# An mLSTM stage whose decay exponents are stored head by head, with their exponentials computed on ScalarE instead of stored and loaded

## The chip, the cores and the metric

The kernel runs on one core of one Trainium2 chip. The metric is the device time of one execution in microseconds (us); a profiled execution has in addition a span, from its first to its last instruction. The engines are named as in the profile: PE is TensorE, PEld its weight loads, DVE is VectorE, ACT is ScalarE, POOL is GpSimd, SP is SyncE (here it only issues DMAs).

## What is computed

One step of a hybrid backbone with a single trunk layer: RMSNorm, one combined input projection, multi-head latent attention beside a bidirectional chunkwise mLSTM, a gated merge, an output projection and a SwiGLU feed-forward part. There are 128 context tokens and 1024 latent tokens, model width 1024. The part that matters here is the mLSTM scan, with 4 heads, key width 128 and value width 256, once forward and once backward:

```python
b = cumsum(fc); log_d = where(mask, b[:, None] - b[None, :] + ic[None, :], -inf)
inter = b + m
m_row = maximum(inter, max(log_d, -1))
d = exp(log_d - m_row)
w_inter = exp(inter - m_row)
s = (q @ k.T) * d
num = s @ v + w_inter * (C @ q)
den = sum(s) + w_inter * (n @ q)
h = num / maximum(abs(den), exp(-m_row))
...
decay = exp(b_last + m - m_new)
C_new = decay * C + einsum(w, v, k)
```

The kernel does this in chunks of 128 tokens. For one token, with the chunk's own running sum taken out, it needs one exponent per head, `N` (minus the row maximum), from which `d` is exp(N + mask + a value per key), and `w_inter` is exp(N + mr), where `mr` is one number per direction, head and chunk.

## The kernel before, in words

All matrices lie transposed, features on partitions. Float32 products that need it are made of three fp32r matmuls (`mm3`, lines 98 to 100), whose high and low parts ACT (`hi`, L69) and DVE (`lo`, L75) split. The program runs through an input stage with 24 big projection tiles (`z_big`), the mLSTM stage (`z2`), the attention, the merge and the feed-forward part. Instructions stand on each engine in the order that the framework's scheduler gave them at build time; each engine works through its list in order and waits where a semaphore isn't there yet. SP's list of DMA issues is in order too.

**The gates** (`gates`, lines 748 to 840) run in the background of the input stage. They hold one row per direction, head and chunk (100 rows with gaps), 128 tokens along the free axis. `N` is computed on DVE (L818), `E` = exp(N + mr) on ACT (L819), and four DMAs (L822) write both for both directions into the DRAM tensor `d_nm`, whose order is [N or E, direction, head, chunk, token]. A diagonal matrix `Z` with the state decay is spread over all partitions by one matmul with ones (L839) and copied to `dec` (L840). `tok` holds other per-token numbers, transposed.

**The mLSTM stage** (`z2`, lines 982 to 1041) takes 18 steps i = 0 to 17, forward and backward chunks in turn; the first two (the context) carry no state in, the other 16 are "carried". Each step has these parts:
- `mload` (L1043), three steps ahead: loads `N` (L1047, one row of 128 tokens per head, spread to all 128 partitions: 256 KB), `S` (L1049: scores and keys, 512 KB), `V` (L1054) at a chunk's first use, and for a carried step `Q` (L1057) and `W` (L1059: the exponentials `E` out of `d_nm`, spread like `N`, 256 KB). The loads of i = 0 are issued by POOL, all others by SP. `N` and `W` have three buffers each.
- `mfront` (L1062), one step ahead: POOL adds the mask to `N` in place (L1072) and multiplies `Q` by `W` (L1074), ACT takes the exponential of `N` for each head (L1077), POOL scales the keys (L1079), DVE multiplies the result by the scores (L1081).
- `mback` (L1084): per head the matmuls L1102 (`N` with `V`), L1104 (`Q` with the state `C`) and L1107 (state update), two instructions each; DVE updates `C` (L1109) and takes the denominators (L1120 to L1122); ACT (L1127, first visit of a chunk) or DVE (L1125, second visit) takes the output out of PSUM.
- `mpost` (L1132): norm, transposes and gating of a finished chunk.

Between these stand pieces of the attention's key, value and query projections (`proj`, `fill`), whose PSUM results ACT copies to `st` tiles (L896, L920, L942). They use two PSUM banks with the tag `mm`. The first `st` tile takes over a buffer from which `z_big` has just stored its last result (`d_z<-zo`, L684).

Of the kernel before, what the change touches and what calls it, by code (L numbers as in the profile page):

```python
# [10 lines left out]
F32 = mybir.dt.float32  # L11
R32 = mybir.dt.float32r
I32 = mybir.dt.int32
AF = mybir.ActivationFunctionType
ALU = mybir.AluOpType
# [4 lines left out]
P = 128  # L20
# [5 lines left out]
NCH = T // P  # L26
CW = 384
CHUNKS = [(i * CW, CW) for i in range(T // CW)]
HM = 4
# [17 lines left out]
NR = 100  # L47
# [9 lines left out]
class K:  # L57
# [107 lines left out]
    def build(self):  # L165
        tc, nc, a, o = self.tc, self.nc, self.a, self.o
        with tc.tile_pool(name="const", bufs=1) as cp, \
                tc.tile_pool(name="dr", bufs=1, space=DRAM) as dp:
            self.cp, self.dp = cp, dp
            self.ident = cp.tile([P, P], F32, name="ident")  # L170
            make_identity(nc, self.ident)
            self.ones = cp.tile([P, P], F32, name="ones")
            nc.gpsimd.memset(self.ones, 1.0)
            self.vec = cp.tile([P, 64], F32, name="vec")
            self.mod1 = cp.tile([P, 16, 2], F32, name="mod1")
            self.mod2 = cp.tile([P, 4, 8, 2], F32, name="mod2")
            self.A1 = cp.tile([P, 8, 2], F32, name="A1")
            self.A2 = cp.tile([P, 8, 2], F32, name="A2")
            self.silc = cp.tile([P, 8, 2], F32, name="silc")
            self.dram()  # L180
            self.bm = cp.tile([P, 48], F32, name="bm")
            self.tok = cp.tile([P, 3, NR], F32, name="tok")
            self.dec = cp.tile([P, NR], F32, name="dec")
            self.inputs()
            self.attention()
            self.merge()
            self.ffn()
# [4 lines left out]
    def dram(self):  # L192
        t = self.dp.tile
        self.d_q = t([NCH, P, HM, P], F32, name="d_q")
        self.d_v = t([NCH, P, HM, DV], F32, name="d_v")
        self.d_s = t([NCH, P, 2, HM * P], F32, name="d_s")
        self.d_sp = t([P, T], F32, name="d_sp")
        self.d_nm = t([2, 2, HM, NCH, P], F32, name="d_nm")
        self.d_lat = t([5, P, T], F32, name="d_lat")
        self.d_z = t([24, P, T], F32, name="d_z")  # L200
        self.d_hm = t([KD, P, T], F32, name="d_hm")
        self.d_qn = t([HA * NOPE, T], F32, name="d_qn")
        self.d_qr = t([HA * ROPE, T], F32, name="d_qr")
        self.d_ko = t([HA * NOPE, NK], F32, name="d_ko")
        self.d_vo = t([HA, P, NCH + 1, AV], F32, name="d_vo")
        self.d_kpe = t([ROPE, T], F32, name="d_kpe")
        self.d_att = [t([P, 2, T], F32, name=f"d_att{k}") for k in range(4)]
        self.d_t2 = t([KD, P, T], F32, name="d_t2")
        self.d_x1 = t([KD, P, T], F32, name="d_x1")
        self.d_w = t([KD // 2, 4, P, HK * P], F32, name="d_w")  # L210
        self.d_g = t([NF, P, T], F32, name="d_g")
# [536 lines left out]
    def gates(self):  # L748


        nc, a, o, pp = self.nc, self.a, self.o, self.pp
        V, S = nc.vector, nc.scalar
# [6 lines left out]
        dirs = ((slice(0, 36), 1, P - 1), (slice(64, 100), -1, 0))  # L759
        I, F, A, U, L, Z, N, E = (g() for _ in range(8))  # L760
        sel, sm, GB, SB = g(17), g(1, 8), g(2), g(18)
        gb, mn, mc = g(18, 8), g(9, 8), g(9, 8)
        mr, nl, dd = g(1), g(1), g(1)
# [6 lines left out]
        for kd, t in enumerate((I, F)):  # L770
            for d in range(2):
                r = 32 * kd + 4 * d
# [43 lines left out]
        V.tensor_scalar(L, F, mr, None, op0=ALU.max)  # L816

        V.tensor_scalar(N, L, -1.0, None, op0=ALU.mult)  # L818
        S.activation(E, N, AF.Exp, bias=mr)  # L819
        for j, t in enumerate((N, E)):  # L820
            for d in range(2):
                nc.sync.dma_start(self.d_nm[j, d].rearrange("h c t -> (h c) t"), t[dirs[d][0]])  # L822
        V.scalar_tensor_tensor(A, A, -1.0, L, op0=ALU.mult, op1=ALU.subtract)
        S.activation(A, A, AF.Exp)
        yield
# [3 lines left out]
        S.activation(U, I, AF.Exp, bias=nl)  # L829
        S.activation(dd, nl, AF.Exp, bias=mr)  # L830
        V.tensor_scalar(Z[:, 0:NR], self.ident[0:NR, 0:NR], dd, None, op0=ALU.mult)
        yield
        yield
        tp = self.bank(pp, "mx")
# [1 line left out]
            nc.tensor.transpose(tp[:, i * NR:(i + 1) * NR], t, self.ident[0:NR, 0:NR])  # L836
        V.tensor_copy(self.tok, tp[:, 0:3 * NR].rearrange("p (g r) -> p g r", g=3))
        db = self.bank(pp, "mx")
        nc.tensor.matmul(db[:, 0:NR], self.ones[0:NR], Z[:, 0:NR], start=True, stop=True)  # L839
        S.copy(self.dec, db[:, 0:NR])  # L840

    def lat_kv(self):

# [199 lines left out]
    def mload(self, i, d, c, carried, second, mp):  # L1043
        nc = self.nc
        eng = nc.gpsimd if i < 1 else nc.sync
        N = mp.tile([P, HM, P], F32, name=self.nm("N"), tag="N", bufs=3)
        eng.dma_start(N, self.d_nm[0, d, :, c].partition_broadcast(P))  # L1047
        S = mp.tile([P, 2, HM * P], F32, name=self.nm("S"), tag="S", bufs=3)
        eng.dma_start(S, self.d_s[c])  # L1049
        Q = W = None  # L1050
        if c not in self.Vt:
            V = self.Vt[c] = mp.tile([P, HM, VW], F32, name=f"V{c}", tag=f"V{c or 3}")
            nc.gpsimd.memset(V[:, :, DV:VW], 1.0)
            eng.dma_start(V[:, :, 0:DV], self.d_v[c])  # L1054
        if carried:
            Q = mp.tile([P, HM, P], F32, name=self.nm("Q"), tag="Q", bufs=3)
            eng.dma_start(Q, self.d_q[c])  # L1057
            W = self.wp.tile([P, HM, P], F32, name=self.nm("W"), tag="ws", bufs=3)
            eng.dma_start(W, self.d_nm[1, d, :, c].partition_broadcast(P))  # L1059
        return S, N, Q, W  # L1060

    def mfront(self, d, c, carried, second, S, E, Q, W):  # L1062

        nc = self.nc
        G = nc.gpsimd
        r = 64 * d + c
        h4 = lambda t: t.rearrange("p (h t) -> p h t", h=HM)
        last = c == (NCH - 1 if d == 0 else 1)
        K = None if last else h4(S[:, 1])

        def work():
            G.tensor_tensor(E, E, self.neg[:, d:d + 1, :].broadcast_to([P, HM, P]), op=ALU.add)  # L1072
            if carried:
                G.tensor_tensor(Q, Q, W, op=ALU.mult)  # L1074
            yield
            for h in range(HM):
                nc.scalar.activation(E[:, h], E[:, h], AF.Exp, bias=self.tok[:, 2, r + 9 * h:r + 9 * h + 1])  # L1077
            if not last:
                G.tensor_tensor(K, K, self.tok[:, 1, r:r + 28:9].unsqueeze(2).broadcast_to([P, HM, P]), op=ALU.mult)  # L1079
            yield  # L1080
            nc.vector.tensor_mul(E, E, h4(S[:, 0]))  # L1081
        return work(), (E, Q, K)

    def mback(self, d, c, carried, second, A, Q, K, C, mp, pp, side, load):  # L1084
# [12 lines left out]
        for h in range(HM):  # L1097
# [7 lines left out]
            if K is not None:  # L1105
                p3 = self.bank(pp, "p3")[:, :VW]
                self.pe = mm(p3, K[:, h], V[:, h], start=True, stop=True).ins  # L1107
                if carried:
                    nc.vector.scalar_tensor_tensor(C[:, r], C[:, r], self.dec[:, r0 + 9 * h:r0 + 9 * h + 1], p3,  # L1109
                                                   op0=ALU.mult, op1=ALU.add)  # L1110
                else:
                    nc.scalar.copy(Co[:, h], p3)
# [983 lines left out]
```

## Time and profile before

| quantity | value |
|---|---|
| time, median of 3 runs (lowest to highest) | 2212.89 us (2212.23 to 2213.59) |
| profiled execution: its own time, and its span | 2207.67 us, 2205.9 us |
| mean granted TensorE clock | 0.967 of 2.4 GHz |
| busy, share of the span: PE, PEld | 93%, 85% |
| busy, share of the span: DVE, POOL, ACT | 69%, 45%, 42% |
| bytes moved by DMA, mean rate | 343.89 MB, 156 GB/s |
| DMA packets, of them under 2 KB | 233794, 166734 |

PE is busy nearly all the time, so time is lost only where PE stands or runs at the lower of its two clock levels. A busy share is a mean over stages: the mLSTM stage, from about 628 to 828 us of the span, has limits of its own. An engine's wait is put down by the trace to the releaser that came last; the DMA engines' share counts the time of packets, and can be a little over 1.

### The profile page before, as it was taken

What the parts mean: (1) busy time and instruction counts of PE and PEld (TensorE: products, weight loads), DVE (VectorE), ACT (ScalarE), POOL (GpSimd) and SP (SyncE); (2) the same over time, 40 slices, a digit from 0 to 9 for tenths busy, and PEclk for the clock granted to TensorE, in tenths of its full rate; (3) what the DMA queues carried; (4) which work ended last, traced back from release to release, by engine and by line L of the source; (5) the groups of instructions that cost most, each with busy time, mean ns of one, the idle gap of its engine ahead of it and who ended that gap; (6) DMA issues with size and microseconds to landing.
All of it is one profiled execution on the core that took longest, in us unless ns stands there. A gap on an engine that the chain in (4) does not pass through costs nothing.

```text
span 2205.9 us, 36808 instructions
## 1 busy us (share of the span) xinstructions
PE 2052.1 (93%) x13495; PEld 1870.1 (85%) x13495; DVE 1531.2 (69%) x2688; ACT 933.2 (42%) x1850; POOL 1002.3 (45%) x774
## 2 busy tenths in 40 slices
PE   5899989999989988999999999889999999989897
PEld 2589989989978775667677899879999999989897
DVE  5737746989844877556665647899655555899895
ACT  4433334455445544333443335544322222456464
POOL 1702223667524414444445535577777733521501
PEclk8899999999999997999999999899999999999899
DMA  7323334555489785222224664223555512557664
GB/s 297 105 96 103 105 104 152 167 164 187 147 264 317 233 265 168 73 69 75 81 75 119 201 207 148 79 88 130 182 178 193 177 61 84 176 166 251 220 200 131
DMA packets 233794, 343.89 MB, mean 156 GB/s; under 512 B 20078, under 2 KB 166734, under 8 KB 232462
## 3 DMA queue, kind: packets, MB, share of 16 engines
q1 hardware_dynamic: 225070, 331.88, 47.1%
q0 software_dynamic: 4848, 6.06, 1.1%
q10 hardware_dynamic: 3696, 3.61, 0.5%
q8 instruction: 106, 1.74, 0.3%
q14 instruction: 74, 0.61, 0.1%
HBM read 253.69 MB, written 87.80 MB: 155 GB/s over the span
## 4 chain that ended last, share of the span: by engine, by line
PE 45%; DVE 12%; DMA 8%; POOL 7%; issue 6%; ACT 2%; SPq 1%; DVEq 0%; POOLq 0%; ACTq 0%
PE mm L98 11%; PE mm L100 11%; PE mm L99 10%; DVE wo L75 4%; PE pv L1476 3%; DMA pr<-w_fo 3%; PE st L98 2%; PE st L99 1%; PE st L100 1%; PE mx L1398 1%; DMA wr<-w_fo 1%; DVE sm L1400 1%; PE p L1102 1%; POOL ps L1773 1%; POOL wm L722 1%
## 5 line engine op out<-in xcount | busy, mean ns | idle before, releaser
L100 PE MATMUL mm<-th,wo 128*128 128x288 f32 x1840 | 546.9, 298 | 14.2 <-DVE wo L75 13.9
L98 PE MATMUL mm<-th,wo 128*128 128x288 f32 x1840 | 547.8, 298 | 2.8 <-DVE zo L1702 1.1
L99 PE MATMUL mm<-tl,wo 128*128 128x288 f32 x1840 | 546.3, 297 | 0.0
L100 PEld LDWEIGHTS mm<-th,wo 128*128 128x128 f32 x1840 | 349.1, 190 | 18.4 <-DVE wo L75 17.9
L75 DVE TENSOR_TENSOR wo<-wr,wo 128x512 fp32r<-128x512 f32 (+1 forms) x317 | 313.1, 1003 | 57.5 <-ACT wo L69 52.9
L98 PEld LDWEIGHTS mm<-th,wo 128*128 128x128 f32 x1840 | 348.4, 189 | 4.8 <-issue 1.9
L99 PEld LDWEIGHTS mm<-tl,wo 128*128 128x128 f32 x1840 | 348.7, 190 | 0.1
L69 ACT ACTIVATE wo<-wr 128x512 fp32r<-128x512 f32 (+1 forms) x317 | 187.5, 608 | 145.8 <-PE mm L100 66.7
L75 DVE TENSOR_TENSOR wo<-ws,wo 128x512 fp32r<-128x512 f32 x188 | 188.2, 1004 | 64.4 <-ACT wo L69 64.3
L69 ACT ACTIVATE wo<-ws 128x512 fp32r<-128x512 f32 x188 | 116.5, 626 | 270.2 <-PE mm L100 152.1
L1445 POOL TENSOR_TENSOR es<-es,p 128x512 f32<-128x512 f32 x112 | 157.3, 1404 | 91.0 <-ACT p L1438 87.0
L100 PE MATMUL mm<-xh,wo 128*128 128x288 f32 x616 | 184.1, 300 | 9.7 <-DVE wo L75 9.7
L98 PE MATMUL mm<-xh,wo 128*128 128x288 f32 x616 | 183.8, 299 | 0.7 <-ACT wo L69 0.7
L99 PE MATMUL mm<-xl,wo 128*128 128x288 f32 x616 | 184.4, 300 | 0.0
L1686 POOL TENSOR_TENSOR ws<-wr,ws 128x512 f32<-128x512 f32 x47 | 62.3, 1326 | 226.1 <-DVE wo L75 220.8
L1438 ACT ACTIVATE p<-st 128x512 f32<-128x512 f32 (+1 forms) x152 | 87.5, 579 | 157.9 <-PE st L100 143.2
L1400 DVE TENSOR_REDUCE sm<-mx 128x1 f32<-128x384 f32 (+1 forms) x200 | 99.2, 540 | 66.1 <-PE mx L1398 65.3
L98 PE MATMUL mm<-B,wo 128*128 128x288 f32 x456 | 134.8, 296 | 2.4 <-DVE zo L1702 1.5
L100 PE MATMUL mm<-B,wo 128*128 128x288 f32 x456 | 134.8, 296 | 0.0
L99 PE MATMUL mm<-B,wo 128*128 128x288 f32 x456 | 134.7, 295 | 0.0
L722 POOL TENSOR_TENSOR wm<-wm,sr 128x512 f32<-128x512 f32 x64 | 100.9, 1579 | 64.6 <-DVE mj L721 61.6
L100 PEld LDWEIGHTS mm<-xh,wo 128*128 128x128 f32 x616 | 117.9, 192 | 11.8 <-DVE wo L75 11.6
(438 smaller groups left out, 5072.9 us busy)
## 6 DMA issues: line engine op xcount, KB each, us to landing
wr<-w_ff SPq DMA_DIRECT2D x56, 512.0 KB
wm<-wm SPq DMA_DIRECT2D x32, 512.0 KB
wr<-d_w SPq DMA_DIRECT2D x32, 512.0 KB
d_z<-zo SPq DMA_DIRECT2D x48, 288.0 KB
d_g<-uu SPq DMA_DIRECT2D x44, 288.0 KB
wr<-w_big SPq DMA_DIRECT2D x24, 512.0 KB
wr<-w_fo SPq DMA_DIRECT2D x24, 512.0 KB
pr<-w_fo SPq DMA_DIRECT2D x40, 256.0 KB
```

Of the source, the lines that this page charges most:

```text
L69: i = self.nc.scalar.activation(out, in_, AF.Copy)
L75: return self.nc.vector.tensor_sub(out, in_, f32v(hi)).ins
L98: mm(out, lhs[0], rhs[0], start=first, stop=False)
L99: mm(out, lhs[0], rhs[1], start=False, stop=False)
L100: self.pe = mm(out, lhs[1], rhs[0], start=False, stop=last).ins
L722: nc.gpsimd.tensor_tensor(w[:, n], w[:, n], sr[:, 1], op=ALU.mult)
L1102: self.pe = mm(p1, A[:, h], V[:, h], start=True, stop=not carried).ins
L1400: self.iv = nc.vector.tensor_reduce(sm[:, t, j:j + 1], s[:, :kc], axis=AX.X, op=ALU.max, negate=True).ins
L1438: self.ia = nc.scalar.activation(p[:, :n], st[:, :n], AF.Exp).ins
L1445: nc.gpsimd.tensor_tensor(U["sum"], U["sum"], p, op=ALU.add)
L1476: self.pe = nc.tensor.matmul(pv[g * AV:(g + 1) * AV, q0:q0 + w], v[:, kb[c]], U["P"][c][:, q0:q0 + w], start=c < 2, stop=c == U["nc"] - 1, ...
L1686: G.tensor_tensor(s4, a12, s2, op=ALU.subtract)
```

## The change

Four things, in one edit:
- `d_nm` becomes [direction, chunk, head, token], `N` alone. Eight DMAs (one per direction and head, 9 rows each) store it instead of four (36 rows each, two for `N` and two for `E`). The load of a step's `N` then reads one run of 2 KB for each partition instead of four of 512 B.
- `E` is no longer computed on ACT in the gates, stored, or loaded. `W` stays as a buffer, without a DMA.
- The gates spread `mr` over the partitions as well: a second diagonal matrix on DVE, a second matmul with ones, and a copy of 200 columns to `dec`, which now has two planes.
- In `mfront` of a carried step, ACT first computes `W` = exp(N + mr) for each of the four heads, from `N` as loaded; the mask is added to `N` in place after that.

```diff
-            self.dec = cp.tile([P, NR], F32, name="dec")
+            self.dec = cp.tile([P, 2, NR], F32, name="dec")
...
-        self.d_nm = t([2, 2, HM, NCH, P], F32, name="d_nm")
+        self.d_nm = t([2, NCH, HM, P], F32, name="d_nm")
...
         V.tensor_scalar(N, L, -1.0, None, op0=ALU.mult)
-        S.activation(E, N, AF.Exp, bias=mr)
-        for j, t in enumerate((N, E)):
-            for d in range(2):
-                nc.sync.dma_start(self.d_nm[j, d].rearrange("h c t -> (h c) t"), t[dirs[d][0]])
+        for d in range(2):
+            for h in range(HM):
+                r = 64 * d + 9 * h
+                nc.sync.dma_start(self.d_nm[d, :, h], N[r:r + NCH])
...
         V.tensor_scalar(Z[:, 0:NR], self.ident[0:NR, 0:NR], dd, None, op0=ALU.mult)
+        V.tensor_scalar(E[:, 0:NR], self.ident[0:NR, 0:NR], mr, None, op0=ALU.mult)
...
-        nc.tensor.matmul(db[:, 0:NR], self.ones[0:NR], Z[:, 0:NR], start=True, stop=True)
-        S.copy(self.dec, db[:, 0:NR])
+        for i, t in enumerate((Z, E)):
+            nc.tensor.matmul(db[:, i * NR:(i + 1) * NR], self.ones[0:NR], t[:, 0:NR], start=True, stop=True)
+        S.copy(self.dec, db[:, 0:2 * NR].rearrange("p (g r) -> p g r", g=2))
...
-        eng.dma_start(N, self.d_nm[0, d, :, c].partition_broadcast(P))
+        eng.dma_start(N, self.d_nm[d, c].partition_broadcast(P))
...
             W = self.wp.tile([P, HM, P], F32, name=self.nm("W"), tag="ws", bufs=3)
-            eng.dma_start(W, self.d_nm[1, d, :, c].partition_broadcast(P))
...
         def work():
+            for h in range(HM if carried else 0):
+                nc.scalar.activation(W[:, h], E[:, h], AF.Exp, bias=self.dec[:, 1, r + 9 * h:r + 9 * h + 1])
             G.tensor_tensor(E, E, self.neg[:, d:d + 1, :].broadcast_to([P, HM, P]), op=ALU.add)
...
-                    nc.vector.scalar_tensor_tensor(C[:, r], C[:, r], self.dec[:, r0 + 9 * h:r0 + 9 * h + 1], p3,
+                    nc.vector.scalar_tensor_tensor(C[:, r], C[:, r], self.dec[:, 0, r0 + 9 * h:r0 + 9 * h + 1], p3,
```

The scheduler makes its lists anew, so the change also moves instructions. After the edit the lines of `mfront` and below have numbers higher by three (L1077 is L1080, L1127 is L1130), those between `gates` and `mload` higher by two (L896 is L898, L1047 is L1049), and the new exponentials are L1074.

The first place is on ACT, where the steps i = 3, 4 and 5 begin (about 664 to 682 us of the trace). The exponents of i = 3, 4, 5 are `N_1030`, `N_1050`, `N_1066` in both programs; `st`, `kc` and `wh` belong to the projections, `h` is a step's output. Before:

```order
L896 COPY kc_1011_6625<-mm_1012_6626 128x128
L896 COPY st_1013_6634<-mm_1014_6635 128x288
L896 COPY st_1013_6634<-mm_1015_6643 128x288
L896 COPY st_1013_6634<-mm_1029_6694 128x288
L1077 ACTIVATE N_1030_6702<-N_1030_6702,tok_95 128x128 x2
L896 COPY st_1013_6634<-mm_1035_6718 128x288
L1077 ACTIVATE N_1030_6702<-N_1030_6702,tok_95 128x128 x2
L69 ACTIVATE wh_1078_6899<-wr_1006_6603 128x512
L896 COPY kc_1039_6747<-mm_1040_6748 128x128
L1077 ACTIVATE N_1050_6784<-N_1050_6784,tok_95 128x128 x4
L1127 ACTIVATE h_1089_6970<-p1_1092_6973,den_1091_6972 128x256 x2
L1127 ACTIVATE h_1089_6970<-p1_1101_7026,den_1091_6972 128x256 x2
```

And now:

```order
L898 COPY kc_1011_6630<-mm_1012_6631 128x128
L1074 ACTIVATE W_1033_6715<-N_1030_6706,dec_96 128x128 x4
L898 COPY st_1013_6639<-mm_1014_6640 128x288
...
L1074 ACTIVATE W_1053_6796<-N_1050_6787,dec_96 128x128 x2
L1080 ACTIVATE N_1030_6706<-N_1030_6706,tok_95 128x128 x4
L1074 ACTIVATE W_1053_6796<-N_1050_6787,dec_96 128x128 x2
L69 ACTIVATE wh_1078_6908<-wr_1006_6608 128x512
L898 COPY kc_1039_6750<-mm_1040_6751 128x128
L1080 ACTIVATE N_1050_6787<-N_1050_6787,tok_95 128x128 x4
L1074 ACTIVATE W_1069_6877<-N_1066_6868,dec_96 128x128 x4
L1130 ACTIVATE h_1089_6979<-p1_1092_6982,den_1091_6981 128x256 x2
L1130 ACTIVATE h_1089_6979<-p1_1101_7038,den_1091_6981 128x256 x2
```

The new exponentials of i = 3 stand ahead of the copies of `st`, two of i = 4 ahead of all four old exponentials of i = 3, and those of i = 5 ahead of the outputs `h`.

The second place is on SP, where the loads of the same steps are issued. Before:

```order
L223 DMA wr_6651<-w_uqn 128x384
L254 DMA d_ko<-st_6538 128x576
L1059 DMA W_6871<-d_nm 128x4x128
L254 DMA d_ko<-st_6538 128x576
L254 DMA d_ko<-kc_6577 128x128
L223 DMA wr_6897<-w_uqr 128x768
L1047 DMA N_6702<-d_nm 128x4x128
L1059 DMA W_6998<-d_nm 128x4x128
L1049 DMA S_6704<-d_s 128x1024
L254 DMA C<-Co_6688 128x1028
L1047 DMA N_6784<-d_nm 128x4x128
L1059 DMA W_7079<-d_nm 128x4x128
```

And now:

```order
L223 DMA wr_6656<-w_uqn 128x384
L254 DMA d_ko<-st_6543 128x576 x2
L254 DMA d_ko<-kc_6582 128x128
L223 DMA wr_6906<-w_uqr 128x768
L1049 DMA N_6706<-d_nm 128x512
L1051 DMA S_6708<-d_s 128x1024
L254 DMA C<-Co_6692 128x1028
L1049 DMA N_6787<-d_nm 128x512
```

The loads of `W` are gone, the loads of `N` are 128 rows of 512 numbers instead of 128 times 4 rows of 128, and the rest keeps its order.

## Rows read from the trace of the kernel before

**Rows 1.** Busy time of the engines in three stretches, with clock and DMA.

```profile
core 0: us, PE busy (x) PEld busy (x) DVE busy (x) ACT busy (x) POOL busy (x), PEclk, DMA share, GB/s
620.00:640.00 20.00, 9.94 (x71) 9.71 (x71) 4.75 (x12) 5.68 (x11) 5.83 (x13) 0.83 0.71 231
640.00:740.00 100.00, 94.69 (x529) 83.94 (x529) 56.09 (x166) 58.22 (x178) 49.86 (x41) 0.98 1.00 323
740.00:800.00 60.00, 53.59 (x293) 45.95 (x291) 52.44 (x181) 34.46 (x109) 15.41 (x15) 0.97 0.64 204
```

**Rows 2.** Chain that ended last, from 625 us: start, us, what.

```profile
629.22 8.96 DMA d_z<-zo
638.33 0.41 ACT st L896
```

**Rows 3.** Timeline, PE, 627 to 684 us: three waits of PE (idle before, releaser).

```profile
638.78 0.61 PE L98 MATMUL mm<-lh,wh 128*128 128x288 f32 x1 [10.06 <-ACT st L896]
...
675.83 0.70 PE L1102 MATMUL p<-V,N 128*128 128x257 f32 x2 [0.85 <-ACT h L1127]
...
682.74 0.67 PE L1102 MATMUL p<-V,N 128*128 128x257 f32 x2 [1.43 <-DVE den L1121]
```

**Rows 4.** DMA in 640 to 740 us: packets, and the loads of W.

```profile
DMA packets 33957, 32.26 MB, mean 323 GB/s; under 512 B 1636, under 2 KB 28894, under 8 KB 33820
...
W<-d_nm SPq DMA_DIRECT2D x12, 256.0 KB
```

**Rows 5.** Waits of POOL, 627 to 800 us: total, times, longest.

```profile
POOL N L1072 <- DMA N<-d_nm: 35.1, 9, 8.0
```

**Rows 6.** DMA in a stretch of 512-byte packets, of 2 KB packets, and in 629 to 633 us.

```profile
DMA packets 1032, 0.52 MB, mean 345 GB/s; under 512 B 31, under 2 KB 1029, under 8 KB 1032
...
DMA packets 292, 0.53 MB, mean 355 GB/s; under 512 B 32, under 2 KB 32, under 8 KB 292
...
DMA packets 823, 0.72 MB, mean 179 GB/s; under 512 B 95, under 2 KB 747, under 8 KB 823
```

**Rows 7.** Line L839 (gates, matmul) and line L822 (gates, stores): ns min/median/max.

```profile
L839 PE MATMUL mx<-g,ones x2: 250/262/273, 337.0 to 337.1; 100*128 100x100 f32 x2
...
L822 SPq DMA_DIRECT2D d_nm<-g x4: 290/330/637, 331.6 to 333.1; - x4
```

**Rows 8.** Timeline, ACT, 664 to 682 us.

```profile
665.00 0.40 ACT L896 COPY st<-mm 128x288 f32<-128x288 f32 x1 [0.16 <-PE mm L100]
...
671.43 1.28 ACT L1077 ACTIVATE N<-N,tok 128x128 f32<-128x128 f32 x4 [2.10 <-POOL N L1072]
674.94 1.57 ACT L1127 ACTIVATE h<-p,den 128x256 f32<-128x256 f32 x4 [2.23 <-DVE den L1120]
679.58 1.28 ACT L1077 ACTIVATE N<-N,tok 128x128 f32<-128x128 f32 x4 [3.07 <-POOL N L1072]
```

**Rows 9.** Timeline, POOL, 665 to 682 us: the mask is added (i = 3, 4, 5).

```profile
665.27 1.29 POOL L1072 TENSOR_TENSOR N<-N,neg 128x512 f32<-128x512 f32 x1 [7.05 <-DMA N<-d_nm]
...
670.12 1.27 POOL L1072 TENSOR_TENSOR N<-N,neg 128x512 f32<-128x512 f32 x1 [0.22 <-DMA N<-d_nm]
...
678.28 1.27 POOL L1072 TENSOR_TENSOR N<-N,neg 128x512 f32<-128x512 f32 x1 [2.14 <-PE p L1107]
```

**Rows 10.** Timeline, SP, 660 to 669 us: issues of W, and of N for i = 5.

```profile
660.16 0.46 SPq L1059 DMA_DIRECT2D W<-d_nm  x1
...
662.62 0.97 SPq L1059 DMA_DIRECT2D W<-d_nm  x1
...
666.42 1.96 SPq L1047 DMA_DIRECT2D N<-d_nm  x1
```

**Rows 11.** Timeline of a later step (i = 11): its exponentials on ACT, its matmuls on PE.

```profile
722.16 1.28 ACT L1077 ACTIVATE N<-N,tok 128x128 f32<-128x128 f32 x4 [3.11 <-POOL N L1072]
...
730.50 0.67 PE L1102 MATMUL p<-V,N 128*128 128x257 f32 x2 [0.55 <-DVE den L1120]
```

**Rows 12.** Waits of PE, 640 to 740 us: total, times, longest.

```profile
PE p L1102 <- DVE y L123: 1.1, 1, 1.1
```

## The prediction, made before the changed kernel ran

> **What bounds the kernel now.** I read the busy shares first: PE has work for 93% of the span, so a change counts only where it takes idle time away from PE or gives it some. Next comes the table of stretches around the mLSTM stage, where all edited lines but the gates work. It shows three different states [rows 1]. From 620 to 640 us PE is busy for 9.94 of 20 us. From 640 to 740 us the DMA engines are full (share 1.00 at 323 GB/s), but PE is busy for 94.69 of 100 us, so the full DMA has cost PE at most 5.3 us there. From 740 to 800 us the DMA share is 0.64 and DVE is busy for 52.44 of 60 us.
>
> The chain of waits tells what the hole before 640 us is: a store of a projection result was issued at 629.22 and took 8.96 us to land, ACT could copy into that buffer only at 638.33 [rows 2], and PE stood for 10.06 us [rows 3]. The waits of POOL tell the rest: it waited 35.1 us in nine pieces for loads of `N` [rows 5]. That looks like much, but POOL works one step ahead of PE. The reader should hold the two beside each other: a late `N` costs only where the chain mask, exponential, product ends later than PE arrives. The timeline shows such a place at i = 5, where PE waited 1.43 us [rows 3], and the opposite at i = 11: its exponentials on ACT were done at 722.16 + 1.28 = 723.4 us, its first matmul ran at 730.50 [rows 11], with 7.1 us between.
>
> **The change, part by part.** All sums are against the profiled execution (2207.67 us, span 2205.9); the median of the runs is 2212.89, 5.2 us above it, and I put the differences on the median.
>
> *Gates.* PE gains two matmuls like the pair of L839, 262 ns each in the median and overlapping [rows 7]: +0.2 us, since PE has no free time at that place. SP gets four more stores of 0.33 us [rows 7], 1.3 us on SP. What stands behind them is weight loads two tiles ahead of their use; if that cover were gone, 1.3 us would be the price. I take 0. The ACT exponential that goes and the small DVE product that comes lie beside PE's work: 0.
>
> *Loads of `W`.* 16 loads of 256 KB go. Twelve of them were issued in the full stretch [rows 4]: 12 x 0.262 = 3.1 of 32.26 MB, so 9.7 of its 100 us of DMA time become free. At a single load of `N` this is worth what stood ahead of it: 0.262 MB at 323 GB/s, 0.8 us for each `W`.
>
> *The stall at 629 us.* The store stands on SP behind one load of `N` and one of `S`, in the same order as before. While these ran, in 629 to 633 us, only 0.72 MB moved, at 179 GB/s [rows 6]; at 345 GB/s it would have taken 2.1 us, not 4. If four times as many packets were the reason, the longer runs give back up to 1.9 us. But 512-byte packets in a filled queue moved at 345 GB/s, 2 KB packets at 355 [rows 6], so packet size alone did not slow a queue. Ends -1.9 and 0; the nearest row is that of the stretch itself, which names no cause, so I take the middle: -0.9. The Trainium skill (page "DMA: Bandwidth & Descriptors", section Specifications) states that line rate is reached from 512 bytes on; by that rule the joined runs bring nothing, this term is 0, and the sum below ends 0.9 us higher. The two rates of the filled queue agree with the rule; the slow stretch is not explained by it.
>
> *Exponentials on ACT.* Four of them last 1.28 us together [rows 8], 16 x 1.28 = 20.5 us in all. ACT has room: 58.22 of 100 us busy, then 34.46 of 60 [rows 1]. Two things are not covered by that. The chain of a carried step gets 1.28 us longer, because the mask may be added only after them; and ACT works in order, so whatever stands behind a new exponential waits with it for `N`.
>
> Where the chain has slack, as at i = 11, the longer chain costs 0. The tight steps are i = 3 to 5:
> - i = 3: its new exponentials stand ahead of the `st` copy that ran at 665.00, and can't start before `N` is there, about 665.27 [rows 8, 9]. They delay it to about 666.5, 1.5 us; PE has two `mm` banks to work in meanwhile, so I take a third: +0.5 (0 to 1.5). Then two new exponentials of i = 4 stand ahead of the old four of i = 3, another 0 to 1.28: I take half, +0.6.
> - i = 4: PE waited 0.85 us there [rows 3]. `N` comes two `W` loads earlier, 1.6 us, and the chain is 1.28 longer: -0.3.
> - i = 5: the mask was added at 678.28 [rows 9]. The two `W` issued ahead of this load [rows 10] are gone, 1.6 us, so take 676.7 for its arrival. The new exponentials last to 678.0, and only then come the outputs `h`, which ran at 674.94 [rows 8] and for whose PSUM banks PE waited until 675.83 [rows 3]. That is 3.1 us more for PE. PE then has the work that it did from 675.83 to 682.74 - 1.43 = 681.31, 5.5 us, and meanwhile the step is ready: its 1.43 us wait falls away. Net +1.7. If `N` came 3 us earlier still, by 673.7, nothing would be held up and the net would be -1.4.
>
> *Later steps.* PE's longest single wait for the rest of the full stretch is 1.1 us, behind DVE rows that themselves stood behind a late product [rows 12]. With less on the DMA queues I give back -0.8 of the 5.3 - 0.85 - 1.43 = 3.0 us left over (ends 0 and -3.0). After 740 us the five steps left bring 6.4 us to ACT, with 25 us free: 0.
>
> Sum: +0.2 - 0.9 + 0.5 + 0.6 - 0.3 + 1.7 - 0.8 = **+1.0 us**, 2213.9 us: no difference that can be told. About 0.2%, 4.4 us, is what a measurement of this kernel can tell from no change, that is 2208.5 to 2217.3.
>
> **The rivals.**
> - *The DMA relief carries through.* `N` arrives before ACT reaches the new exponentials, so nothing is held up, the 5.3 us of PE's idle time in the full stretch goes, and the stall loses its 1.9: -7.2 + 0.2 = -7.0, 2205.9 us. For it: the DMA share of 1.00 and the 35.1 us for which POOL waited. Against it: PE has so little idle time there, and the releasers that PE names are mostly DVE and ACT.
> - *ACT is held up again and again* (slower). What I find at i = 5 repeats: a new exponential waits for `N` and the PSUM copies behind it leave PE without banks. Five further steps of the full stretch at +1.7 each give +8.5, 2213.9 + 8.5 = 2222.4 us. It decides itself by whether `N` lands later than the moment at which ACT has finished what stands ahead. For it: nine waits for `N` of 3.9 us on average. Against it: steps with 7 us of slack, and one to two fewer loads ahead of each `N`.
> - *The change doesn't do what it says*: `N` still moves in packets of 512 bytes, because the run of 2 KB is cut up. Then only the bytes of `W` count, the stall stays, and the sum is +1.9: 2214.8 us.
>
> **How the numbers follow.** My forecast gets 0.39, the relief 0.33, the held-up ACT 0.25, the packets that stay small 0.03. The relief is faster by more than 4.4 us, the held-up ACT slower; the forecast, whose terms reach about 3 us to either side, lies within 0.2% but for 0.02 on the slow side; so does the last rival. That gives faster 0.33, same 0.40, slower 0.27. The likeliest case's own range is 2211 to 2217 us. As it holds less than half, the range for 8 times in 10 takes in most of both rivals: 2203 (the relief with 3 us more, from the idle time after 740 us) to 2222 (where the held-up ACT is cut near its middle).
>
> **What would show it.** Right: a PE gap near 629 us of 8 to 10 us; no `W` packets and a DMA share under 1 between 640 and 740 us; a longer PE wait for the `h` of i = 3 where `N` of i = 5 comes in; ACT waits put down to `N<-d_nm`, not to POOL. Wrong: PE busy over 98 of the 100 us (the relief), PE waits for ACT lines of 1 to 3 us at many steps (the held-up ACT), or a gap at 629 us that is gone, which none of my terms holds.

## The result, and the profile after

The change is slower by a little: median 2217.11 us (20 runs, 2210.86 to 2220.05) against 2212.53 us for the kernel before in the same comparison. The ratio is 1.0023, 95% interval 1.0016 to 1.0029, so +5.1 us (3.5 to 6.4). The forecast was +1.0 us. The interval lies across the 0.2% that the prediction called no difference; the time is inside the range of 2203 to 2222 us and past the end, by a hair, of the likeliest case's own 2211 to 2217.

The table of stretches of the kernel after (columns as in [rows 1]):

```profile
core 0: us, PE busy (x) PEld busy (x) DVE busy (x) ACT busy (x) POOL busy (x), PEclk, DMA share, GB/s
620.00:640.00 20.00, 11.69 (x89) 11.46 (x87) 5.74 (x15) 3.89 (x7) 6.25 (x14) 0.90 0.53 181
640.00:740.00 100.00, 92.78 (x501) 81.47 (x502) 47.30 (x144) 70.49 (x217) 44.58 (x39) 0.95 0.90 289
740.00:800.00 60.00, 53.96 (x292) 46.35 (x290) 56.32 (x174) 39.27 (x125) 19.75 (x17) 0.97 0.57 175
```

The DMA relief came (share 1.00 to 0.90), ACT took on 12.3 us, and PE is busy for 92.78 instead of 94.69 us [rows 1], at a lower clock. The stall before the stage did not change, 10.1 us against 10.06 [rows 3]. From the waits of PE, 640 to 740 us, and then 740 to 840 us (engine, line, releaser: total, times, longest):

```profile
PE mm L98 <- ACT st L898: 11.2, 3, 10.1
PE mm L98 <- ACT st L922: 1.9, 2, 1.7
PE p L1105 <- DVE N L1084: 0.9, 1, 0.9
...
PE p L1110 <- DVE C L1112: 3.7, 3, 1.8
PE mm L98 <- ACT zq L69: 2.1, 1, 2.1
```

And the waits of POOL and of ACT, 627 to 800 us:

```profile
POOL N L1075 <- ACT W L1074: 33.2, 13, 6.5
POOL N L1075 <- DMA N<-d_nm: 3.3, 1, 3.3
...
ACT W L1074 <- DMA N<-d_nm: 8.3, 8, 2.3
```

Where POOL waited 35.1 us for loads [rows 5], it now waits 33.2 us for the new exponentials, and ACT waits 8.3 us for the loads in its place. What that does to PE can be read at i = 11. Timeline of ACT, then of PE:

```profile
719.85 1.28 ACT L1074 ACTIVATE W<-N,dec 128x128 f32<-128x128 f32 x4 [1.24 <-DMA N<-d_nm]
721.04 0.35 ACT L922 COPY st<-mm 128x256 f32<-128x256 f32 x1
722.52 1.28 ACT L1080 ACTIVATE N<-N,tok 128x128 f32<-128x128 f32 x4 [1.14 <-POOL N L1075]
723.71 0.35 ACT L922 COPY st<-mm 128x256 f32<-128x256 f32 x1
...
720.08 0.59 PE L1105 MATMUL p<-V,N 128*128 128x257 f32 x2
...
724.11 0.39 PE L98 MATMUL mm<-wh,lh 128*128 128x256 f32 x1 [1.71 <-ACT st L922]
...
725.95 1.06 PE L1105 MATMUL p<-V,N 128*128 128x257 f32 x2
```

ACT waits for `N`, then for the mask that POOL could add only after the new exponentials; the copy of `st` stands behind both, and PE waits 1.71 us for its bank. The masked exponentials of i = 11 ran at 722.16 before [rows 11] and run at 722.52 now, so the step itself was not late: the copy behind it was. The new exponentials look like the cause; run e10 below has the same wait without them.

After that wait the clock fell to its lower level, 1.2 GHz: the pair of L1105 takes 1.06 us behind it and 0.59 ahead of it. Stretches of the clock in the kernel after, one behind each of the PE waits of 1.7, 1.8 and 2.1 us:

```profile
724.70:728.10 3.40, 3.40 (x12) 2.75 (x11) 0.48 (x1) 2.62 (x9) 1.05 (x2) 0.50 0.50 170
775.90:779.30 3.40, 3.01 (x8) 2.48 (x9) 3.40 (x8) 2.60 (x8) 1.65 (x2) 0.50 0.37 105
806.60:810.00 3.40, 3.10 (x13) 2.69 (x13) 2.16 (x12) 3.27 (x12) 0.00 (x0) 0.50 0.44 136
```

In each, PE does in 3.4 us what takes 1.7 us at full clock. Between 650 us and the attention the kernel before has one such stretch, and the kernel after these three. The one of before:

```profile
790.10:793.50 3.40, 3.40 (x9) 2.67 (x9) 3.40 (x15) 0.88 (x2) 0.00 (x0) 0.50 1.08 365
```

Not every wait of this length is followed by such a stretch. The kernel before stood 1.74 us ahead of a matmul at 818.47 us, and its clock stayed at 1.00 to 828 us; what decides between the two isn't shown here. The matmul, and the stretch around it:

```profile
818.47 1.09 PE L1148 MATMUL mm<-ident,h 128*128 128x128 f32 x8 [1.74 <-ACT st L942]
...
816.00:828.00 12.00, 9.12 (x65) 7.70 (x64) 6.15 (x10) 1.47 (x4) 0.80 (x1) 1.00 1.07 333
```

How far behind is it, and where? PE's order is new as well, so steps can be compared only where the same number of matmuls stands ahead. Counted from step 0, that holds at i = 4 (100 matmuls in both), at i = 12 (335) and at the first matmul of the attention. Microseconds from the end of the stall to these points, one profile of each:

| | to i = 4 | to i = 12 | to the attention |
|---|---|---|---|
| before | 37.1 | 100.2 | 189.5 |
| after | 39.4 | 103.4 | 196.1 |

So +2.3 us by i = 4, +0.9 from there to i = 12, +3.4 after that: +6.6 in the stage, somewhat more than the +5.1 of the medians. (These two profiled executions are 9.2 us apart, 2216.86 against 2207.67 us, and in the change the stall ended 3 us later, at 641.83 us.) The whole stage, before and then after, in one row each:

```profile
638.78:828.28 189.50, 173.19 (x989) 152.00 (x990) 126.29 (x391) 103.56 (x313) 67.68 (x58) 0.98 0.88 282
...
641.83:837.95 196.12, 178.41 (x989) 154.79 (x990) 127.58 (x391) 123.16 (x377) 66.13 (x57) 0.96 0.80 255
```

PE is idle for 17.7 us instead of 16.3. The kernel before has other waits in place of the long ones of the change, so only 1.4 of the 6.6 us are more waiting. The other 5.2 are longer busy time for the same work: the two further stretches at 1.2 GHz account for 3.4 of them, and for the last 1.8 no cause is shown.

### The profile page after: what moved, and what is told of

It is laid out like the page before. It is cut to its first block, busy times and chain, and to the rows that moved or that the text cites. A ratio compares the mean times of both kernels' runs of the same rounds, so it can differ in the third digit from the quotient of the medians.

```text
span 2215.0 us, 36852 instructions
## 1 busy us (share of the span) xinstructions
PE 2057.4 (93%) x13497; PEld 1868.9 (84%) x13497; DVE 1531.5 (69%) x2689; ACT 953.7 (43%) x1913; POOL 1001.6 (45%) x774
## 3 DMA queue, kind: packets, MB, share of 16 engines
q8 instruction: 106, 1.74, 0.3%
## 4 chain that ended last, share of the span: by engine, by line
PE 43%; DVE 13%; DMA 8%; issue 7%; POOL 6%; ACT 2%; SPq 1%; DVEq 0%; POOLq 0%; ACTq 0%
PE mm L98 10%; PE mm L100 10%; PE mm L99 10%; DVE wo L75 5%; PE pv L1479 3%; DMA pr<-w_fo 3%; PE st L98 2%; PE st L99 1%; PE st L100 1%; PE mx L1401 1%; DVE sm L1403 1%; POOL ps L1776 1%; POOL wm L722 1%; PE p L1105 1%; POOL ps L1779 1%
```

## The experiments

Three theories. **Held-up ScalarE**: the new exponentials wait for `N`, or lengthen the chain, and what stands behind them waits too. **Layout**: packets decide. **New lists**: the scheduler, given other work, put all engines' instructions in another order, and that order costs. All ratios are against the kernel before, run on the same chip beside them; in microseconds, 0.001 is 2.2. "Stage" is the time from the end of the stall to the first matmul of the attention, in one profile. A median is over 8 to 12 executions, but over five for e9 and six for e10. A profile is one execution: that of e2 was 7.2 us above its median and that of e6 4.0 us below, so a stage time alone settles nothing smaller than that.

| run | order of the stage | median us | ratio (95%) | stage us |
|---|---|---|---|---|
| before | its own | 2210.0 to 2212.5 | 1 | 189.5 |
| the change | new | 2217.11 | 1.0023 (1.0016 to 1.0029) | 196.1 |
| e1_layout | as before | 2208.21 | 0.9984 (0.9975 to 0.9994) | 188.2 |
| e2_act_short_runs | new | 2216.72 | 1.0030 (1.0017 to 1.0043) | 197.8 |
| e3_no_w | new | 2213.19 | 1.0007 (0.9998 to 1.0017) | 190.1 |
| e4_before_plus_exps | new | 2214.06 | 1.0019 (1.0009 to 1.0029) | 196.1 |
| e5_swap | new | 2219.03 | 1.0031 (1.0020 to 1.0042) | 198.1 |
| e6_one_exp | new | 2218.05 | 1.0030 (1.0018 to 1.0041) | 192.0 |
| e7_one_exp_swap | new | 2216.31 | 1.0024 (1.0015 to 1.0034) | 194.8 |
| e8_free_exps | new | 2208.09 | 0.9984 (0.9975 to 0.9993) | 189.5 |
| e9_after_in_before_lists | as before | 2225.58 | 1.0068 (1.0055 to 1.0081) | 200.0 |
| e10_before_in_after_lists | as the change | 2217.52 | 1.0036 (1.0022 to 1.0051) | 196.4 |
| e11_no_w_in_before_lists | as before | 2206.00 | 0.9981 (0.9972 to 0.9989) | 185.4 |
| e12_one_exp_last_in_before_lists | as before (POOL free) | 2210.18 | 1.0001 (0.9993 to 1.0010) | 190.8 |

**The parts of the change alone.** The layout, with `N` and `W` both stored head by head and both loaded (the stores and the load of `N` are edited in the same way):

```diff
-        self.d_nm = t([2, 2, HM, NCH, P], F32, name="d_nm")
+        self.d_nm = t([2, 2, NCH, HM, P], F32, name="d_nm")
...
-            eng.dma_start(W, self.d_nm[1, d, :, c].partition_broadcast(P))
+            eng.dma_start(W, self.d_nm[1, d, c].partition_broadcast(P))
```

> The layout alone: N and E both stored head by head and loaded in runs of 2 KB, W still loaded, no new exponential on ScalarE. Held-up ScalarE (the loss of the change comes from the new exponentials standing ahead of other work): within 2 us of the kernel before, ratio 0.999 to 1.001, and the stall near 629 us stays at about 10 us, as it did with the change. Layout (the eight small stores or the long runs cost the time): as slow as the change, +4 to +5 us, ratio 1.002. New lists (any edit that makes the scheduler write its lists anew can move the time by some us): off by 3 us or more to either side.

0.9984, faster by 3.5 us; no complete version is better (e8 equals it). Of the theories only the new lists allowed for that much, but the order of the stage is that of the kernel before save for a few neighbours, so they don't explain it. In the full stretch DMA moved 335 GB/s, with 323 before [rows 1], and POOL's waits for `N` (627 to 800 us) fell from 35.1 us [rows 5]:

```profile
640.00:740.00 100.00, 97.82 (x544) 88.51 (x544) 57.18 (x169) 59.63 (x179) 47.56 (x41) 0.96 0.99 335
...
POOL N L1074 <- DMA N<-d_nm: 25.1, 8, 6.4
```

By its one profile the stage is only 1.3 us shorter than before, so how the gain comes about is not shown.

The change with short runs (`d_nm` as [direction, head, chunk, token]):

```diff
-        self.d_nm = t([2, NCH, HM, P], F32, name="d_nm")
+        self.d_nm = t([2, HM, NCH, P], F32, name="d_nm")
```

> The exponentials alone: W computed on ScalarE and no longer loaded, but N still stored by four rows a head and loaded in runs of 512 bytes. Held-up ScalarE: as slow as the change, +3 to +6 us, ratio about 1.002. Layout: no slower than before, within 2 us. New lists: anything within 5 us of before, not tied to the change.

1.0030: within the intervals as slow as the change. The loss isn't the layout's.

No `W` at all:

```diff
-                G.tensor_tensor(Q, Q, W, op=ALU.mult)
+                G.tensor_tensor(Q, Q, Q, op=ALU.mult)
```

> Leaves out the factor w_inter: W is neither loaded nor computed, Q is multiplied by itself in its place, so POOL has the same work and ScalarE none of the new; the layout and the gates are those of the change. It shows the DMA relief alone. Held-up ScalarE: faster than the kernel before by 2 to 7 us, ratio 0.997 to 0.999, with PE idle for less than 5 us in the first 100 us of the stage. New lists or layout: within 2 us of before, or slower.

1.0007: a miss for the relief. With less work than e1 it was slower than e1, which pointed to the order. The exponentials alone, on top of the kernel before:

```diff
         def work():
+            for h in range(HM if carried else 0):
+                nc.scalar.activation(self.scr, E[:, h], AF.Exp, bias=self.dec[:, r + 9 * h:r + 9 * h + 1])
```

> The kernel before, with W loaded as ever, and in addition four exponentials of N per carried step into a scratch tile that nobody reads, ahead of the mask as in the change. ScalarE's work and the longer chain without the DMA relief. Held-up ScalarE: slower than the change, +6 to +10 us, ratio 1.003 to 1.0045. New lists or layout: within 3 us of before.

1.0019, nearly the whole loss, with `W` still loaded: less than held-up ScalarE expected, and more than the 3 us of the other two theories. So the exponentials, or the order that the scheduler makes around them, are the cause.

**Which property of the exponentials?** Their place, their length, or their need of `N`. First the place (`X` is multiplied by the scores and goes to the matmuls, `E` now multiplies `Q`):

```diff
+        X = W if carried else E
...
-            for h in range(HM if carried else 0):
-                nc.scalar.activation(W[:, h], E[:, h], AF.Exp, bias=self.dec[:, 1, r + 9 * h:r + 9 * h + 1])
-            G.tensor_tensor(E, E, self.neg[:, d:d + 1, :].broadcast_to([P, HM, P]), op=ALU.add)
+            G.tensor_tensor(X, E, self.neg[:, d:d + 1, :].broadcast_to([P, HM, P]), op=ALU.add)
             yield
...
+            for h in range(HM if carried else 0):
+                nc.scalar.activation(E[:, h], E[:, h], AF.Exp, bias=self.dec[:, 1, r + 9 * h:r + 9 * h + 1])
```

> The change with the order of the two kinds of exponentials turned round: the mask is added into the W tile, the four masked exponentials work there and come first, and the four exponentials of N follow in place in N and multiply Q. ScalarE has the same instructions; the chain load of N, mask, masked exponentials is as long as before the change. Longer chain (the loss sits in the wait of the mask behind the four new exponentials): ratio 0.998 to 1.000 to the kernel before, stage like that before (188 to 190 us). ScalarE's time itself (the four instructions push the evictions that lie behind them, wherever they stand): ratio 1.0015 to 1.003, stage 194 to 198 us.

1.0031: putting them behind the masked ones saved nothing. And among ACT's waits from 627 to 800 us there is none for a load of `N` any more, so that wait is not what costs the time here. One exponential in the place of four (0.63 us instead of 1.28):

```diff
+        V.tensor_scalar(F, L, -1.0, mr, op0=ALU.mult, op1=ALU.add)
...
-                nc.sync.dma_start(self.d_nm[d, :, h], N[r:r + NCH])
+                nc.sync.dma_start(self.d_nm[d, :, h], F[r:r + NCH])
...
-            for h in range(HM if carried else 0):
-                nc.scalar.activation(W[:, h], E[:, h], AF.Exp, bias=self.dec[:, 1, r + 9 * h:r + 9 * h + 1])
+            if carried:
+                nc.scalar.activation(W, E, AF.Exp)
```

> The change, but N is stored with the running maximum already added, and the masked exponentials' bias has it taken off; so W is one exponential of 128x512 with no bias per carried step, in the place of four of 128x128. ScalarE's time of the new exponentials falls to about half of 1.28 us a step. ScalarE's time: half of the loss is left, ratio about 1.001, stage about 192 us. Longer chain: the mask waits half as long, also about 1.001; a loss that stays whole (1.002) would speak for the wait on N as such, whatever the exponentials take.

1.0030: halving them saved nothing either. Both edits at once:

> Both edits together: one exponential of 128x512 per step, and it comes behind the four masked ones. Longer chain: 0.998 to 1.000, as with the turned order alone. ScalarE's time: about 1.001, as with the one exponential alone. If both count, this is the fastest of the four and stands near the layout alone (0.998).

1.0024, a miss; here too ACT has no wait for a load of `N`. And the same work on ACT, but of a constant:

```diff
-                nc.scalar.activation(self.scr, E[:, h], AF.Exp, bias=self.dec[:, r + 9 * h:r + 9 * h + 1])
+                nc.scalar.activation(self.scr, self.ident, AF.Exp, bias=self.dec[:, r + 9 * h:r + 9 * h + 1])
```

> The kernel before with four exponentials of a constant 128x128 tile per carried step ahead of the mask, written to a scratch tile: the same time on ScalarE as with the scratch exponentials of N (ratio 1.0019), but they wait for no load and no one waits for them. ScalarE's time itself: again about 1.002. Waiting for N (instructions on ScalarE stuck behind an exponential whose N hasn't come): 1.000.

0.9984: 26 us of extra ACT time (64 x 408 ns) brought no loss. The group of these instructions (count, busy us, mean ns, idle before) and the stretch:

```profile
L1074 ACT ACTIVATE scr<-ident,dec 128x128 f32<-128x128 f32 x64 | 26.1, 408 | 0.9
```

```profile
640.00:740.00 100.00, 95.30 (x535) 85.10 (x536) 56.80 (x169) 74.81 (x232) 47.77 (x40) 0.98 0.99 322
```

ACT is busier here than in the change (74.81 against 70.49 us), and PE loses nothing. But the test is weaker than it was meant to be. Nothing holds these instructions at their steps, and all 64 ran from 629 to 684 us, while the new exponentials of the change run from 645 to 778 us. So it says that ACT had 26 us free early in the stage, and nothing about the later steps. And each of these kernels has an order of its own, which had to be held still.

**The order held still.** A table gives, for each engine, the stage's instructions in the order of one kernel, and draws an edge from each to the next:

```diff
+            for p, q in zip(seq, seq[1:]):
+                self.tc.add_manual_dep(q, p.name, mybir.DependencyInfo(mybir.DependencyClass.NoSync, mybir.DependencyReason.DATA),
+                                       reason="in_order")
```

> The change, with every instruction of the mLSTM stage on TensorE, VectorE, ScalarE, GpSimd and SyncE held in the order of the kernel before (a table of that order, drawn as edges between neighbours on an engine); only the new exponentials are put in where the scheduler finds room. New lists (the loss is the order that the scheduler chose anew, not the work): ratio 0.997 to 0.999, at or below the layout alone. Exponentials that wait for N (their own cost, in any order): 1.002 to 1.003, as with the change.

1.0068: +15 us, which neither theory expected. In the old order the change is not harmless but three times as dear. Waits of POOL, then of ACT, 627 to 800 us:

```profile
POOL N L1136 <- ACT W L1135: 59.0, 13, 8.6
...
POOL Q L1138 <- ACT W L1135: 21.3, 2, 19.1
...
ACT W L1135 <- DMA N<-d_nm: 15.8, 9, 3.0
```

ACT stood 15.8 us for `N`, nearly twice the 8.3 of the change, and POOL 80.3 us for the exponentials. By i = 4 the stage is 9.3 us behind the kernel before (46.4 against 37.1), with PE's order the same, and at its end 10.5. So nearly all that the stage loses is lost early, around POOL's one wait of 19.1 us. Timeline of POOL around it, in the kernel before and then here:

```profile
648.96 1.27 POOL L1074 TENSOR_TENSOR Q<-Q,W 128x512 f32<-128x512 f32 x1 [0.72 <-DMA Q<-d_q]
654.35 1.27 POOL L1074 TENSOR_TENSOR Q<-Q,W 128x512 f32<-128x512 f32 x1 [4.12 <-DMA Q<-d_q]
...
672.55 1.27 POOL L1138 TENSOR_TENSOR Q<-Q,W 128x512 f32<-128x512 f32 x1 [19.14 <-ACT W L1135]
675.95 1.27 POOL L1138 TENSOR_TENSOR Q<-Q,W 128x512 f32<-128x512 f32 x1 [2.13 <-ACT W L1135]
677.21 1.26 POOL L1136 TENSOR_TENSOR N<-N,neg 128x512 f32<-128x512 f32 x1
```

The old order has the products `Q` times `W` of i = 3 and 4 ahead of the mask of i = 3, because there `W` came by a load of its own, earlier than `N`. Now `W` is made from `N`, and the mask waits behind both products: it is added at 677.21, where the kernel before added it at 665.27 [rows 9]. The new exponentials of i = 3 ran at 671.18 without a wait for the load. So this loss points to an order that doesn't fit the work more than to ACT's waits for loads; that is read from one profile, and no run tests it by itself.

> The reverse: the kernel before, its stage held in the order of the change (without the new exponentials, which it doesn't have; its W loads are put in where the scheduler finds room). New lists: slower although no work was added, ratio 1.0015 to 1.003. Exponentials that wait for N: 0.999 to 1.000.

1.0036: the order of the change costs 8 us (5 to 11) with the work of the kernel before, which has none of the new exponentials. Four waits of PE that the change has stand here at the same matmuls: 0.77 us for the product of i = 3 (0.88 in the change), 1.59 for `st` (1.71), 1.61 for `C` (1.80) and 1.62 for `zq` (2.12); a second wait for `zq` is longer here. Timeline of PE, then of ACT and POOL around the second of them, and the waits for `zq`:

```profile
672.34 0.67 PE L1163 MATMUL p<-V,N 128*128 128x257 f32 x2 [0.77 <-DVE N L1142]
722.47 0.38 PE L143 MATMUL mm<-wh,lh 128*128 128x256 f32 x1 [1.59 <-ACT st L965]
772.73 0.70 PE L1168 MATMUL p<-V,S 128*128 128x257 f32 x2 [1.61 <-DVE C L1170]
801.87 0.86 PE L143 MATMUL mm<-zq,wh 128*128 128x288 f32 x2 [1.62 <-ACT zq L114]
...
720.88 1.28 ACT L1138 ACTIVATE N<-N,tok 128x128 f32<-128x128 f32 x4 [3.37 <-POOL N L1133]
722.07 0.35 ACT L965 COPY st<-mm 128x256 f32<-128x256 f32 x1
...
719.57 1.28 POOL L1133 TENSOR_TENSOR N<-N,neg 128x512 f32<-128x512 f32 x1 [3.38 <-DMA N<-d_nm]
...
PE mm L143 <- ACT zq L114: 4.1, 2, 2.5
```

At i = 11 the mask itself waits for the load of `N`, and the copy of `st` stands behind the masked exponentials because the new order has it there. So the wait of 1.71 us that was followed above comes with the order and not with the new exponentials. From the end of the stall to i = 4, i = 12 and the attention it is 39.1, 106.4 and 196.4 us here, against 39.4, 103.4 and 196.1 in the change. One thing is not held still: the loads of `W`, which that order doesn't have, were put in by the scheduler. No engine's wait is put down to one of them.

> The kernel with no W at all (Q times Q stands for Q times W, so the factor w_inter is left out) in the order of the kernel before: layout and DMA relief with neither exponentials nor a new order. New lists: the run without W lost to the layout alone by its order, so this one stands at 0.998 or below, and what it gains over 0.9984 is the relief of the DMA queues (0 to -3 us). If it stays at 1.0007, the order is not what cost there, and N landing earlier or missing W loads are.

0.9981: what e3 lost against it, 0.0026 or 5.7 us, was its order alone, since the work is the same. Against e1 the missing `W` loads bring 0.0003, 0.7 us, inside the intervals, although DMA is relieved in the same stretch:

```profile
640.00:740.00 100.00, 96.33 (x543) 87.08 (x544) 59.82 (x169) 60.23 (x181) 46.85 (x43) 0.97 0.94 310
```

The last one is meant to remove both the wait and the order: one exponential per step, pinned behind the masked ones, in the old order. POOL's order is left to the scheduler, since the product with `W` now comes later there.

```diff
+                one = nc.scalar.activation(E, E, AF.Exp).ins
...
+                self.tc.add_manual_dep(one, four.name, mybir.DependencyInfo(mybir.DependencyClass.NoSync, mybir.DependencyReason.DATA),
+                                       reason="in_order")
```

> A last version of the change that leaves nothing out: one exponential of 128x512 per carried step, which stands on ScalarE directly behind the four masked ones (so N is known to be there and ScalarE never waits for a load on its account), with TensorE, VectorE, ScalarE and SyncE in the order of the kernel before. Both causes together (ScalarE standing for N in the old order, and the scheduler's new order elsewhere): both are gone, so the time is that of the kernel without W in the old order plus a little for 16 longer steps, ratio 0.998 to 1.000. If ScalarE's added work as such is what costs, in whatever place: 1.002 or more.

1.0001, just past the slow end of what was expected: about 5 us better than the change, level with the kernel before, 4.4 us behind e11. It does the work of e7, which had cost 1.0024 in an order of the scheduler's. Waits of POOL, 627 to 800 us:

```profile
POOL Q L1136 <- ACT N L1134: 14.6, 7, 2.4
POOL W L1132 <- DMA N<-d_nm: 9.7, 3, 4.4
```

No ACT wait for `N` is left, and POOL adds the mask of i = 3 ahead of the product of i = 3. So e12 differs from e9 in several things, and doesn't say which of them brought the 15 us. The version that beats both kernels is e1: the layout without the exponentials.

**What is shown and what is open.** Shown: the order that the scheduler made for the change costs 8 us without the new exponentials (e10), with PE's long waits at the same matmuls; a new order also cost e3 5.7 us (against e11), and e5 and e7 are as slow as the change though ACT never waits for a load of `N` in them. In the change, exponentials and order together cost 9.3 us (against e11, by the ratios), so about 1 us is left for the exponentials themselves, less than the intervals can tell from nothing. The layout gives 3.5 us back and the relief 0.7. The change in the old order costs 19 us more than e11 (e9; 14.6 of them in the stage by the two profiles), but there POOL stands in an order made for loaded `W`. A new order need not be worse: e8's has none of the loss. Open: what exponentials that wait for `N` on ACT cost by themselves, since no run has that wait alone; how the layout brings its gain; why one order is good and another not, beyond the waits named here; and whether an order exists in which the change beats e1, which wasn't tried.

## Why the prediction came out as it did

The sum was +1.0 and the result +5.1 us: the direction was right, and some 4 us were missing. That the sign came out right is luck: the sum's largest positive term did not happen, and what cost the time, the order of the lists, was in none of its terms. Of the signs of being right, the gap of 10.1 us, the lower DMA share and ACT's waits for `N` came; the longer wait for the `h` of i = 3 did not. Term by term, by the profiles:

- *Stall at 629 us*, -0.9: it was 0. The store took 9.23 us to land after, 8.96 before [rows 2], and PE's wait stayed at 10.1 us (in the chain of the kernel after: start, us, what):

```profile
632.05 9.23 DMA d_z<-zo
```

  The rule in the Trainium skill ("DMA: Bandwidth & Descriptors", Specifications) that line rate is reached from 512 bytes on, by which this term is 0, was the better guide here; taking the middle of two ends was the error. By that rule e1, whose work is that of the kernel before and whose lists nearly are, should bring nothing either, and it brought 3.5 us, with 335 instead of 323 GB/s in the full stretch: there the measurement decides, and the sum had no term for it.
- *i = 3 and 4*, +0.5 + 0.6 - 0.3: right in place, too small, and in part not for the reason given. PE waited 0.40 us for `st` and 0.88 us for the product of i = 3 where the text said, and the stage is 2.3 us behind at i = 4. But e10 has 0.77 us of the second wait and is 2.0 us behind there without the new exponentials.
- *i = 5*, +1.7: did not happen. Its exponentials ran at 678.36 without a wait for `N`, the outputs `h` behind them, and PE did not wait for them. Timeline of the kernel after for these three steps, PE and then ACT:

```profile
671.16 0.40 PE L98 MATMUL mm<-lh,wh 128*128 128x288 f32 x1 [0.40 <-ACT st L898]
676.15 0.67 PE L1105 MATMUL p<-V,N 128*128 128x257 f32 x2 [0.88 <-DVE N L1084]
...
678.36 1.26 ACT L1074 ACTIVATE W<-N,dec 128x128 f32<-128x128 f32 x4
679.74 1.64 ACT L1130 ACTIVATE h<-p,den 128x256 f32<-128x256 f32 x4
```

- *Later steps*, -0.8: the relief may be worth that (0.7 us, e11 against e1, inside the intervals), but the term left out the other side. It and the next one are the step that failed: both take the lists of the kernel before, add the new exponentials, and put what the new lists do elsewhere at nothing. "Where the chain has slack, as at i = 11, the longer chain costs 0" held for the chain, with 7.1 us of slack. But the copy of `st` stands behind that step's exponentials in the new order, and PE lost 1.71 us to it, as it does in e10 without a longer chain (1.59 us). I checked whether the step was late and not who stood behind it on ACT, though the text had named just that danger.
- *After 740 us*, 0 because ACT has 25 us free: +3.4 from i = 12 to the attention. Two of the three long PE waits lie here, for `C` and for `zq`, and both are in e10 too (1.61 and 1.62 us), so they come with the order; ACT's free time had no part in it.

Of the rivals, *ACT is held up again and again* came nearest in kind: ACT waited eight times for `N`, 1.0 us on average, and a copy of `st` behind exponentials did leave PE without a bank. But PE waits about as long where there are no new exponentials (e10). So its price, +8.5 us, is near the 9.3 us of exponentials and order by coincidence: 8 of them come with the order. What kept the result at 5.1 is the layout, 3.5 us, and the relief, 0.7. The *DMA relief* rival fell: e11 gives its true size. Packets did grow, so the third rival fell as well. That the scheduler's new order has a cost of its own, on engines and steps that the edit doesn't touch, was in none of the cases; I read the new lists only at i = 3 to 5.

## What to carry to other kernels

When a scheduler rebuilds its lists, an edit is not measured alone: hold the order still (edges between neighbours do it) and run old work in the new order and new work in the old one before believing in either. A wait behind the edited instructions is not yet their price: here four waits of PE looked like it, and stood at the same matmuls without them. New work in the old order needs the same care, since an order made for a value that was loaded early can block an engine once that value is computed late (19.1 us of POOL in e9). And to test a step for slack, look at what stands behind it on its engine in the new lists, not only at its own consumer.

## What the runs showed that was not expected

- A full DMA (share 1.00) that PE hardly feels: with the loads of `W` gone and the order held, the time fell by 0.7 us, where an estimate from the bytes of `W` had 9.7 us of DMA time becoming free.
- Three PE waits of 1.7 to 2.1 us in the change were each followed by 3.4 us at 1.2 GHz, while one of 1.74 us in the kernel before was not. The two stretches that the change has more make up 3.4 us of its loss in the stage, against 1.4 us of added waiting.
- One exponential of 128x512 takes 0.63 us, four of 128x128 take 1.28 us, and that difference of 0.65 us in 16 steps showed nowhere in the time (e6 against the change, each in an order of its own).
